# A decoder layer on one Trainium2 core: the indexer's small products on 64 rows, a weight split moved among the keys, a row sum moved ahead of a split

## The chip, the cores and the metric

The kernel runs on one core of one Trainium2 chip. The metric is device time in microseconds (us) of one execution; lower is better. The profile is that of one execution, taken by the hardware profiler. The engines are PE (TensorE, matrix products; PEld is its loading of weights), DVE (VectorE), ACT (ScalarE), POOL (GpSimd) and SP (SyncE, which issues the weights' transfers).

## The reference

One layer of a hybrid decoder on 256 tokens with 16 meta tokens ahead of them (T = 272), width 2048, all in float32. The parts that the change touches are the indexer, the keys and values, and the FFN's down projection with the last norm:

```python
q, c_kv, q_idx, k_idx, w_idx, u = split_columns(h @ w_in[l])
c_kv = rms_norm(c_kv, kv_norm_g[l])
...
dots = jnp.einsum('bqhd,bsd->bqhs', qi, k_idx)            # 16 indexer heads of 64
score = jnp.einsum('bqhs,bqh->bqs', jax.nn.relu(dots), wi)
_, sel = lax.top_k(score, top_k)                          # 64 of 272 keys
...
h = layer_norm(ALPHA * h + mix, ln1_g[l], ln1_b[l])
f = conv_gated_ffn(h, w_up[l], conv_w[l], conv_b[l], w_down[l])
h = layer_norm(ALPHA * h + f, ln2_g[l], ln2_b[l])
```

Attention then runs over the selected keys, and a causal pooling runs beside it; neither is touched.

## The kernel before

**Products in two parts.** Each fp32 operand is split into an upper part (rounded to fp32r, copied by ACT) and a lower part (the rest, subtracted by DVE). A product is three matmuls: upper weights by upper data (L199), upper by lower (L200) and lower by upper (L201), added up in PSUM. `product` issues them for 16 slices k of 128 rows.

**Weights.** The list `stream` (L92 to L104) holds all weight tiles of 128 x 2048 in the order of their use: eight tiles of the indexer's queries (two heads of 64 per tile), w_uk, w_uv, sixteen more projections, w_o, and the FFN's tiles by a plan; the last four are tiles of w_down (`spare` is the first of them, `last` the last). `weights(ahead=2)` hands out the next tile and calls `prefetch`, which calls `emit` (L135 to L158) for tiles two further on; `fetch` (L110 to L129) issues the transfer on SP and splits the tile in halves: ACT's upper (L127), DVE's lower (L128). The raw and the split tiles are in pools of three. Each engine works in the order in which its instructions are issued; where that isn't enough, `tc.issue_after` (in `behind`, L171 to L176) puts an instruction behind another one.

**Start.** 13 matmuls on zeros (L85 to L89; the zeros come from POOL) run while the first data comes. x and the first weights come in slices k, each split by ACT and DVE (L222 to L225), and L264 to L270 multiply them into three PSUM banks: indexer key and head weights (80 columns), and the two halves of the latent.

**Indexer.** The key of 64 rows is copied to both halves of `kidx`'s 128 rows (L273 to L279): slice 0 is the upper part on both halves, slices 1 and 2 are zero but for the lower part on one half each. The queries of a tile's two heads lie so (L383, L384) that head i has its upper part on half i of the rows and its lower part on the other half. One matmul of 128 rows with slice 0 therefore gives upper by upper and lower by upper, and one with slice 1 + i gives upper by lower:

```python
for o, n, t in ((pa_[:, S * i:S * i + S], S, slice(0, P)), (pb[:, :T], T, slice(P, S))):
    nc.tensor.matmul(o, qi[:, i, t], kidx[:, 0, :n], start=True, stop=False)
    nc.tensor.matmul(o, qi[:, i, t], kidx[:, 1 + i, :n], start=False, stop=True)
```

The queries are in two blocks of 128; the first sees 256 keys at most, the second 272. `dots(j)` does two heads; it is issued inside the product of the next tile, one head behind slice 9 and the other behind slice 12 (L369 to L385). ACT's relu and DVE's weighted sum turn it into `score`.

**Keys and values.** L394 to L403 multiply w_uk's tile with the latent into eight keys, each evicted by ACT (L401); dots(7) stands behind the third key. L407 to L439 multiply w_uv's tile into the values (L426 to L431). w_uv's tile is split like any other, two tiles ahead. DVE's top-k follows (L442 to L452).

**Last stage.** The last four tiles of w_down are split, and `row_sums` (L185 to L191) adds each raw tile's rows on ACT, in place, and splits the sum into two further columns of the split tile, from which PE makes the mean. L907 to L909 issue the row sums of the first three of them behind the third one's split. L984 to L1008 multiply the four tiles into pieces of the output: in each piece first tile 0, then tile 3, then tiles 1 and 2; the piece from 1792 on (MEAN) takes the sums' columns along. The partial results of the tiles before are added to y by DVE (L843), and L915 sums y.

Of the kernel before, what the change touches and what calls it, by code (L numbers as in the profile page):

```python
# [23 lines left out]
NQ = T - Q0  # L24
KT = D // P
# [4 lines left out]
DI = 64  # L30
# [13 lines left out]
KA = NM + P  # L44
# [24 lines left out]
def tile_layer(ctx, tc, xt, w_first, w_proj, w_uk, w_uv, w_pool, w_o, w_up, w_down, cols, rows, rel_bias, onehot, out):  # L69
    nc = tc.nc  # L70
# [10 lines left out]
    def small():  # L81
        return pa.tile([P, 512], F32, tag="at", name="at")


    warm = sb.tile([P, 256], mybir.dt.bfloat16, name="warm")  # L85
    nc.gpsimd.memset(warm, 0.0)
    ps = small()
    for _ in range(13):
        nc.tensor.matmul(ps[:, :256], warm[:, :P], warm, start=True, stop=True)  # L89


# [3 lines left out]
    kinds = {}  # L95
# [11 lines left out]
    ready, raws, split = {}, {}, {}  # L107
    state = {"next": 0, "use": 0}

    def fetch(raw, hl, src, kind, front):  # L110
# [15 lines left out]
        for c in (slice(a, b) for a, b in zip(cuts, cuts[1:])):  # L126
            upper = nc.scalar.activation(hl[:, 0, c], raw[:, c], AF.Copy)  # L127
            lower = nc.vector.tensor_tensor(hl[:, 1, c], raw[:, c], hl[:, 0, c].bitcast(F32), op=ALU.subtract)  # L128
        return tuple(getattr(ins, "ins", ins) for ins in (upper, lower))  # L129

    def weight_tiles():
        raw = wp.tile([P, 2048], F32, tag="wraw", name="wraw")
# [2 lines left out]
    def emit(i):  # L135
        if i in ready:
            return
        if i == last:

            raw = wp.tile([P, 2048], F32, tag="wraw", name="wraw")  # L140
            nc.sync.dma_start(raw, stream[i])
            raws[i] = raw
            ready[i] = []
            for c in range(0, 2048, 256):
                hl = ring.tile([P, 2, 258], F32R, tag="act", name="whl_r", padded_shape=[P, 2, T])
                nc.scalar.activation(hl[:, 0, :256], raw[:, c:c + 256], AF.Copy)
                nc.vector.tensor_tensor(hl[:, 1, :256], raw[:, c:c + 256], hl[:, 0, :256].bitcast(F32), op=ALU.subtract)
                ready[i].append(hl)
            return
        if i == spare:  # L150
            raw = wp.tile([P, 2048], F32, tag="wraw", name="wraw")
            hl = sb.tile([P, 2, 2048 + 2], F32R, tag="y", name="whl_y")
        else:
            raw, hl = weight_tiles()
        split[i] = fetch(raw, hl, stream[i], kinds.get(i), i and split[i - 1][1])
        ready[i] = hl
        if i >= spare:
            raws[i] = raw  # L158

# [25 lines left out]
    def row_sums(i, hl):  # L185

        total = sb.tile([P, 1], F32, name=f"total{i}")
        nc.scalar.activation(raws[i], raws[i], AF.Copy, accum_out=total)
        hi, lo = (hl[-1][:, p, 256:] if isinstance(hl, list) else hl[:, p, 2048:] for p in range(2))
        nc.scalar.activation(hi, total.to_broadcast([P, 2]), AF.Copy)  # L190
        nc.vector.tensor_tensor(lo, total.to_broadcast([P, 2]), hi.bitcast(F32), op=ALU.subtract)  # L191

    def product(ps, hl, m, act, lo, hi, ks=range(KT), width=P, k0=0, k1=KT):

        for n in range(k0, k1):
            k = ks[n]
            wh, wl = hl[:, 0, k * width:k * width + m], hl[:, 1, k * width:k * width + m]
            ah, al = act[k][:, 0, lo:hi], act[k][:, 1, lo:hi]
            nc.tensor.matmul(ps, wh, ah, start=n == 0, stop=False)  # L199
            nc.tensor.matmul(ps, wh, al, start=False, stop=False)  # L200
            nc.tensor.matmul(ps, wl, ah, start=False, stop=n == KT - 1)  # L201
# [61 lines left out]

    heads = [(big(), a, m) for a, m in ((0, 80), (80, P), (80 + P, P))]  # L264
    for k, (hl, a0) in enumerate(first):
        for ps, a, m in heads:
            wh, wl = hl[:, 0, a0 + a:a0 + a + m], hl[:, 1, a0 + a:a0 + a + m]
            nc.tensor.matmul(ps[:m, :T], wh, x_parts[k][:, 0, :], start=k == 0, stop=False)  # L268
            nc.tensor.matmul(ps[:m, :T], wh, x_parts[k][:, 1, :], start=False, stop=False)  # L269
            nc.tensor.matmul(ps[:m, :T], wl, x_parts[k][:, 0, :], start=False, stop=k == KT - 1)  # L270
    ps = heads[0][0]

    kidx = ap_.tile([P, 3, T], F32R, name="kidx", tag="kidx")  # L273
    nc.gpsimd.memset(kidx[:, 1:, :].bitcast(F32), 0.0)
    for r0 in (0, DI):
        nc.scalar.activation(kidx[r0:r0 + DI, 0, :], ps[:DI, :T], AF.Copy)
    for i in range(2):
        nc.vector.tensor_tensor(kidx[DI * i:DI * i + DI, 1 + i, :], ps[:DI, :T], kidx[:DI, 0, :].bitcast(F32),
                                op=ALU.subtract)  # L279
# [22 lines left out]
    ps = small()  # L302
# [46 lines left out]
            nc.gpsimd.dma_start(dst, src)  # L349


    def dots(j, qi, pa_, heads):

        for i in heads:
            h = 2 * j + i
            pb = small()
            for o, n, t in ((pa_[:, S * i:S * i + S], S, slice(0, P)), (pb[:, :T], T, slice(P, S))):
                nc.tensor.matmul(o, qi[:, i, t], kidx[:, 0, :n], start=True, stop=False)  # L358
                nc.tensor.matmul(o, qi[:, i, t], kidx[:, 1 + i, :n], start=False, stop=True)
# [9 lines left out]
    for j in range(8):  # L369
        hl = weights()  # L370
        ps = big()
        product(ps[:, :S], hl, P, x_parts, NM, T, k1=9)
        if j:
            pa_ = small()
            dots(j - 1, qis[j - 1], pa_, (0,))
        product(ps[:, :S], hl, P, x_parts, NM, T, k0=9, k1=12)
        if j:
            dots(j - 1, qis[j - 1], pa_, (1,))
        product(ps[:, :S], hl, P, x_parts, NM, T, k0=12)
        qi = queries[:, j % 2]  # L380
        for i in range(2):
            r, o = slice(DI * i, DI * i + DI), slice(DI - DI * i, 2 * DI - DI * i)
            nc.scalar.activation(qi[r, i, :], ps[r, :S], AF.Copy)  # L383
            nc.vector.tensor_tensor(qi[o, i, :], ps[r, :S], qi[r, i, :].bitcast(F32), op=ALU.subtract)  # L384
# [9 lines left out]
    for h in range(H):  # L394
        ps = small()
        for c in range(2):
            w = slice(1024 * c + h * HD, 1024 * c + h * HD + HD)
            nc.tensor.matmul(ps[:, :T], uk[:, 0, w], ctp[:, c, 0, :], start=c == 0, stop=False)
            nc.tensor.matmul(ps[:, :T], uk[:, 0, w], ctp[:, c, 1, :], start=False, stop=False)
            nc.tensor.matmul(ps[:, :T], uk[:, 1, w], ctp[:, c, 0, :], start=False, stop=c == 1)  # L400
        nc.scalar.activation(kt[:, h, :], ps[:, :T], AF.Copy)  # L401
# [515 lines left out]
    def piece(i, q):  # L917
        a, b = cuts[i][q]
# [165 lines left out]
```

## Time and profile before

| | |
|---|---|
| median of 3 runs | 1043.34 us (1043.13 to 1043.67) |
| the profiled execution | 1043.2 us, its span 1041.3 us |
| granted clock of PE, mean | 0.998 |
| ACT's splits of weights (L127) | 416, 402.8 us |
| DVE's lower parts (L128) | 416, 486.3 us |
| DMA | 250.28 MB, mean 240 GB/s |

The page gives each engine's busy time and its share of the span, then a chain of work that ended last, followed back from the end. A row of the timeline has the start in us from the span's start, the duration in us, the engine, the line, the operation, what it writes and reads, the shape, and how many instructions it stands for; behind these, in brackets, how long the engine stood idle before it and what ended that. A matmul's shape 128*128 128x256 is weights of 128 rows and 128 columns by data of 128 rows and 256 columns. Matmuls overlap in the pipeline and their ends are modelled, so the distance between two starts is the better measure of one matmul's slot.

### The profile page before, as it was taken

What the parts mean: (1) busy time and instruction counts of PE and PEld (TensorE: products, weight loads), DVE (VectorE), ACT (ScalarE), POOL (GpSimd) and SP (SyncE); (2) the same over time, 40 slices, a digit from 0 to 9 for tenths busy, and PEclk for the clock granted to TensorE, in tenths of its full rate; (3) what the DMA queues carried; (4) which work ended last, traced back from release to release, by engine and by line L of the source; (5) the groups of instructions that cost most, each with busy time, mean ns of one, the idle gap of its engine ahead of it and who ended that gap; (6) DMA issues with size and microseconds to landing.
All of it is one profiled execution on the core that took longest, in us unless ns stands there. A gap on an engine that the chain in (4) does not pass through costs nothing.

```text
span 1041.3 us, 19198 instructions
## 1 busy us (share of the span) xinstructions
PE 1033.3 (99%) x7643; PEld 984.3 (95%) x7643; DVE 891.0 (86%) x1401; ACT 621.0 (60%) x1000; POOL 189.5 (18%) x246
## 2 busy tenths in 40 slices
PE   9999999999999999999999999999999999999997
PEld 9999999999999999999999999999999999999986
DVE  6879568758779998888999999989998999999876
ACT  7656446645439855555665556555556565565665
POOL 1200014125330021130121111211112101120031
PEclk9999999999999999999999999999999999999999
DMA  9755543354553578879887788877988778887865
GB/s 326 259 187 218 214 142 131 134 200 165 176 189 131 197 223 240 278 282 302 274 277 261 269 297 276 276 263 267 296 271 285 264 274 285 279 273 271 288 215 160
DMA packets 59754, 250.28 MB, mean 240 GB/s; under 512 B 21734, under 2 KB 22416, under 8 KB 32656
## 3 DMA queue, kind: packets, MB, share of 16 engines
q1 hardware_dynamic: 34592, 230.42, 61.2%
q0 software_dynamic: 7888, 16.14, 8.3%
q10 hardware_dynamic: 17184, 2.49, 1.4%
q8 instruction: 60, 0.98, 0.4%
q14 instruction: 30, 0.25, 0.1%
HBM read 232.50 MB, written 2.11 MB: 225 GB/s over the span
## 4 chain that ended last, share of the span: by engine, by line
PE 89%; DVE 5%; issue 3%; ACT 1%; POOL 1%; DMA 1%; POOLq 0%; DVEq 0%; ACTq 0%
PE mm L200 22%; PE mm L199 22%; PE mm L201 22%; PE at L786 6%; PE at L785 6%; PE at L787 6%; DVE whl L128 2%; DMA wraw<-in_w_down 1%; PE mm L268 1%; PE mm L269 1%; PE mm L270 1%; ACT whl L127 1%; DVE x L701 0%; DVE hp L706 0%; PE at L358 0%
## 5 line engine op out<-in xcount | busy, mean ns | idle before, releaser
L128 DVE TENSOR_TENSOR whl<-wraw,whl 128x1024 fp32r<-128x1024 f32 (+1 forms) x416 | 486.3, 1203 | 37.7 <-ACT whl L127 36.8
L127 ACT ACTIVATE whl<-wraw 128x1024 fp32r<-128x1024 f32 (+1 forms) x416 | 402.8, 1015 | 98.6 <-PE mm L201 21.7
L200 PE MATMUL mm<-hp,whl 128*128 128x258 f32 x1280 | 362.4, 283 | 0.1
L199 PE MATMUL mm<-hp,whl 128*128 128x258 f32 x1280 | 361.4, 282 | 0.0
L201 PE MATMUL mm<-hp,whl 128*128 128x258 f32 x1280 | 361.2, 282 | 0.0
L200 PEld LDWEIGHTS mm<-hp,whl 128*128 128x128 f32 x1280 | 242.7, 190 | 3.3 <-DVE hp L706 0.3
L199 PEld LDWEIGHTS mm<-hp,whl 128*128 128x128 f32 x1280 | 242.5, 189 | 3.3
L201 PEld LDWEIGHTS mm<-hp,whl 128*128 128x128 f32 x1280 | 242.9, 190 | 0.2
L199 PE MATMUL mm<-xp,whl 128*128 128x256 f32 (+5 forms) x384 | 111.9, 291 | 0.0
L200 PE MATMUL mm<-xp,whl 128*128 128x256 f32 (+5 forms) x384 | 108.7, 283 | 0.0
L201 PE MATMUL mm<-xp,whl 128*128 128x256 f32 (+5 forms) x384 | 108.7, 283 | 0.0
L720 ACT ACTIVATE z<-mm,cv 128x256 f32<-128x256 f32 x40 | 22.6, 564 | 100.9 <-PE mm L201 100.9
L757 POOL TENSOR_TENSOR forms<-za 128x128 f32<-128x128 f32 x20 | 21.9, 1095 | 309.6 <-DVE za L738 243.1
L720 ACT ACTIVATE za<-mm,cv 128x256 f32<-128x256 f32 x40 | 22.6, 565 | 85.5 <-PE mm L201 77.4
L199 PEld LDWEIGHTS mm<-xp,whl 128*128 128x128 f32 x384 | 72.4, 189 | 1.0 <-issue 0.5
L200 PEld LDWEIGHTS mm<-xp,whl 128*128 128x128 f32 x384 | 72.3, 188 | 0.4
L201 PEld LDWEIGHTS mm<-xp,whl 128*128 128x128 f32 x384 | 72.4, 189 | 0.3 <-DVE whl L128 0.2
L786 PE MATMUL at<-whl,gp 128*128 128x512 f32 x180 | 71.1, 396 | 0.0
L787 PE MATMUL at<-whl,gp 128*128 128x512 f32 x180 | 71.0, 395 | 0.0
L785 PE MATMUL at<-whl,gp 128*128 128x512 f32 x180 | 69.3, 395 | 0.0
L760 POOL TENSOR_TENSOR forms<-za 128x128 f32<-128x128 f32 x20 | 22.6, 1131 | 199.0 <-DVE za L738 185.4
L787 PEld LDWEIGHTS at<-whl,gp 128*128 128x128 f32 x180 | 33.8, 188 | 7.9
(348 smaller groups left out, 1918.2 us busy)
## 6 DMA issues: line engine op xcount, KB each, us to landing
wraw<-in_w_up SPq DMA_DIRECT2D x88, 1024.0 KB, 5.0
wraw<-in_w_down SPq DMA_DIRECT2D x80, 1024.0 KB, 6.2
wraw<-in_w_proj SPq DMA_DIRECT2D x24, 1024.0 KB, 5.1
wraw<-in_w_o SPq DMA_DIRECT2D x16, 1024.0 KB, 4.9
y<-v POOLq DMA_DIRECT2D x27, 256.0 KB, 8.2
y<-u POOLq DMA_DIRECT2D x18, 256.0 KB, 4.9
wraw<-in_w_first SPq DMA_DIRECT2D x8, 304.0 KB, 5.4
x<-in_xt SPq DMA_DIRECT2D x1, 2176.0 KB, 8.4
```

The lines of the kernel that those rows point to most:

```text
L127: upper = nc.scalar.activation(hl[:, 0, c], raw[:, c], AF.Copy)
L128: lower = nc.vector.tensor_tensor(hl[:, 1, c], raw[:, c], hl[:, 0, c].bitcast(F32), op=ALU.subtract)
L199: nc.tensor.matmul(ps, wh, ah, start=n == 0, stop=False)
L200: nc.tensor.matmul(ps, wh, al, start=False, stop=False)
L201: nc.tensor.matmul(ps, wl, ah, start=False, stop=n == KT - 1)
L268: nc.tensor.matmul(ps[:m, :T], wh, x_parts[k][:, 0, :], start=k == 0, stop=False)
L720: nc.scalar.activation(z, src[:, 2:NQ], AF.Identity, bias=col(C_B, j), scale=col(C_W, 3 * j + 2))
L757: nc.gpsimd.tensor_tensor(s[:, 0], a21, a22, op=ALU.add)
L760: nc.gpsimd.tensor_tensor(s[:, 3], a11, a21, op=ALU.subtract)
L785: nc.tensor.matmul(ps, a[:, 0, i], hl[:, 0, w], start=j == 0, stop=False)
L786: nc.tensor.matmul(ps, a[:, 0, i], hl[:, 1, w], start=False, stop=False)
L787: nc.tensor.matmul(ps, a[:, 1, i], hl[:, 0, w], start=False, stop=j == n - 1)
```

## The change

- **Indexer.** `kidx` has two slices, upper and lower, both filled on both halves. `dots` takes four PSUM banks, issues the four upper products on 128 rows and then four lower products on 64 rows each, the first head's on rows 0 to 63 and the second's on rows 64 to 127. Both heads stand behind slice 9 of the next tile. dots(7) takes its banks from the other pool.
- **Values' weights.** At w_uv's place in the stream only its transfer is issued. Its split is done in halves, behind the evictions of the second and the fourth key; the keys' evictions stand behind the last query's.
- **Row sum.** The row sum of the first of the last four tiles is issued ahead of the second tile's split, which is put behind it; the sums over y stand behind the last row sum.
- **Start.** The warm-up reads a constant of the program, not POOL's zeros, and has 14 matmuls. For the first four slices the three banks' products are ordered by kind: all upper by upper, then upper by lower, then lower by upper.

The diff, without the lines that only pass these things on:

```diff
-    warm = sb.tile([P, 256], mybir.dt.bfloat16, name="warm")
-    nc.gpsimd.memset(warm, 0.0)
+    warm = nc.const_aps.tensor(1.0, (P, 256), mybir.dt.bfloat16)
     ps = small()
-    for _ in range(13):
+    for _ in range(14):
...
+    def split_part(raw, hl, c, after=()):
+        with ExitStack() as edges:
+            for ins in after:
+                edges.enter_context(tc.issue_after(ins))
+            upper = nc.scalar.activation(hl[:, 0, c], raw[:, c], AF.Copy)
+        lower = nc.vector.tensor_tensor(hl[:, 1, c], raw[:, c], hl[:, 0, c].bitcast(F32), op=ALU.subtract)
+        return tuple(getattr(ins, "ins", ins) for ins in (upper, lower))
...
-        split[i] = fetch(raw, hl, stream[i], kinds.get(i), i and split[i - 1][1])
         ready[i] = hl
+        if i == VALUES:
+
+            nc.sync.dma_start(raw, stream[i])
+            held.extend((raw, hl))
+            return
+        if i == spare + 1:
+
+            with behind(spare):
+                sums = row_sums(spare, ready[spare])
+            split[i] = fetch(raw, hl, stream[i], None, 0, (sums,))
+        else:
+            split[i] = fetch(raw, hl, stream[i], kinds.get(i), i and i - 1 in split and split[i - 1][1])
...
-        for ps, a, m in heads:
-            wh, wl = hl[:, 0, a0 + a:a0 + a + m], hl[:, 1, a0 + a:a0 + a + m]
-            nc.tensor.matmul(ps[:m, :T], wh, x_parts[k][:, 0, :], start=k == 0, stop=False)
-            nc.tensor.matmul(ps[:m, :T], wh, x_parts[k][:, 1, :], start=False, stop=False)
-            nc.tensor.matmul(ps[:m, :T], wl, x_parts[k][:, 0, :], start=False, stop=k == KT - 1)
+
+        terms = [(t, h) for h in heads for t in range(3)]
+        if k < 4:
+            terms.sort(key=lambda x: x[0])
+        for t, (ps, a, m) in terms:
+            nc.tensor.matmul(ps[:m, :T], hl[:, t // 2, a0 + a:a0 + a + m], x_parts[k][:, t % 2, :],
+                             start=k == 0 and t == 0, stop=k == KT - 1 and t == 2)
...
-    kidx = ap_.tile([P, 3, T], F32R, name="kidx", tag="kidx")
-    nc.gpsimd.memset(kidx[:, 1:, :].bitcast(F32), 0.0)
+    kidx = ap_.tile([P, 2, T], F32R, name="kidx", tag="kidx")
...
+    for r0 in (0, DI):
+        nc.vector.tensor_tensor(kidx[r0:r0 + DI, 1, :], ps[:DI, :T], kidx[:DI, 0, :].bitcast(F32), op=ALU.subtract)
...
-    def dots(j, qi, pa_, heads):
-
-        for i in heads:
+    def dots(j, qi, buffer=small):
+
+
+        ps = [[buffer(), buffer()] for _ in range(2)]
+
+        blocks = ((S, slice(0, P)), (T, slice(P, S)))
+        for i2, (n, t) in enumerate(blocks):
+            for i in range(2):
+                nc.tensor.matmul(ps[i2][i][:, :n], qi[:, i, t], kidx[:, 0, :n], start=True, stop=False)
+        for i2, (n, t) in enumerate(blocks):
+            for i in range(2):
+                r = slice(DI * i, DI * i + DI)
+                nc.tensor.matmul(ps[i2][i][:, :n], qi[r, i, t], kidx[r, 1, :n], start=False, stop=True)
+        for i in range(2):
             h = 2 * j + i
-            pb = small()
-            for o, n, t in ((pa_[:, S * i:S * i + S], S, slice(0, P)), (pb[:, :T], T, slice(P, S))):
-                nc.tensor.matmul(o, qi[:, i, t], kidx[:, 0, :n], start=True, stop=False)
-                nc.tensor.matmul(o, qi[:, i, t], kidx[:, 1 + i, :n], start=False, stop=True)
             rl = temp([P, KW], "rl")
-            nc.scalar.activation(rl[:, :KA], pa_[:, S * i:S * i + KA], AF.Relu)
-            nc.scalar.activation(rl[:, KA:], pb[:, :T], AF.Relu)
             for i2, (a, b) in enumerate(((0, KA), (KA, KW))):
+                nc.scalar.activation(rl[:, a:b], ps[i2][i][:, :b - a], AF.Relu)
...
         product(ps[:, :S], hl, P, x_parts, NM, T, k1=9)
         if j:
-            pa_ = small()
-            dots(j - 1, qis[j - 1], pa_, (0,))
-        product(ps[:, :S], hl, P, x_parts, NM, T, k0=9, k1=12)
-        if j:
-            dots(j - 1, qis[j - 1], pa_, (1,))
-        product(ps[:, :S], hl, P, x_parts, NM, T, k0=12)
+            dots(j - 1, qis[j - 1])
+        product(ps[:, :S], hl, P, x_parts, NM, T, k0=9)
...
-        nc.scalar.activation(kt[:, h, :], ps[:, :T], AF.Copy)
+        with tc.issue_after(query):
+            key = nc.scalar.activation(kt[:, h, :], ps[:, :T], AF.Copy)
         if h == 2:
-            dots(7, qis[7], small(), (0, 1))
+            dots(7, qis[7], big)
+        if h in (1, 3):
+
+            split_part(*held, slice(512 * h - 512, 512 * h + 512), (getattr(key, "ins", key),))
...
     with behind(spare + n - 2):
-        for k in range(n - 1):
-            row_sums(spare + k, hls[k])
+        for k in range(1, n - 1):
+            of_weights = row_sums(spare + k, hls[k])
...
     for i in range(2):
-        nc.scalar.activation(y2[:, i], y2[:, i], AF.Copy, accum_out=mvs[i][:, 0:1])
+        with tc.issue_after(of_weights):
+            nc.scalar.activation(y2[:, i], y2[:, i], AF.Copy, accum_out=mvs[i][:, 0:1])
```

More of the change, by code (lines that the diff above doesn't have):

```diff
@@ L106, in tile_layer, with fetch @@
     spare, last = len(stream) - PARTS[-1], len(stream) - 1
-    ready, raws, split = {}, {}, {}
+    VALUES = stream.index(w_uv)
+    ready, raws, split, held = {}, {}, {}, []
     state = {"next": 0, "use": 0}
-    def fetch(raw, hl, src, kind, front):
+    def split_part(raw, hl, c, after=()):
[5 more added lines that the diff above has]
+        return tuple(getattr(ins, "ins", ins) for ins in (upper, lower))
+    def fetch(raw, hl, src, kind, front, after=()):
         nc.sync.dma_start(raw, src)
@@ L125, in fetch @@
             cuts = (0, 1024, 1536)
[L126 to L129, printed above, removed]
+        for a, b in zip(cuts, cuts[1:]):
+            parts = split_part(raw, hl, slice(a, b), after)
+        return parts
     def weight_tiles():
@@ L189, in row_sums @@
         hi, lo = (hl[-1][:, p, 256:] if isinstance(hl, list) else hl[:, p, 2048:] for p in range(2))
-        nc.scalar.activation(hi, total.to_broadcast([P, 2]), AF.Copy)
+        upper = nc.scalar.activation(hi, total.to_broadcast([P, 2]), AF.Copy)
         nc.vector.tensor_tensor(lo, total.to_broadcast([P, 2]), hi.bitcast(F32), op=ALU.subtract)
+        return getattr(upper, "ins", upper)
     def product(ps, hl, m, act, lo, hi, ks=range(KT), width=P, k0=0, k1=KT):
@@ L265, in tile_layer @@
     for k, (hl, a0) in enumerate(first):
-        for ps, a, m in heads:
-            wh, wl = hl[:, 0, a0 + a:a0 + a + m], hl[:, 1, a0 + a:a0 + a + m]
-            nc.tensor.matmul(ps[:m, :T], wh, x_parts[k][:, 0, :], start=k == 0, stop=False)
-            nc.tensor.matmul(ps[:m, :T], wh, x_parts[k][:, 1, :], start=False, stop=False)
-            nc.tensor.matmul(ps[:m, :T], wl, x_parts[k][:, 0, :], start=False, stop=k == KT - 1)
+        terms = [(t, h) for h in heads for t in range(3)]
[4 more added lines that the diff above has]
+                             start=k == 0 and t == 0, stop=k == KT - 1 and t == 2)
     ps = heads[0][0]
-    kidx = ap_.tile([P, 3, T], F32R, name="kidx", tag="kidx")
-    nc.gpsimd.memset(kidx[:, 1:, :].bitcast(F32), 0.0)
+    kidx = ap_.tile([P, 2, T], F32R, name="kidx", tag="kidx")
     for r0 in (0, DI):
         nc.scalar.activation(kidx[r0:r0 + DI, 0, :], ps[:DI, :T], AF.Copy)
-    for i in range(2):
-        nc.vector.tensor_tensor(kidx[DI * i:DI * i + DI, 1 + i, :], ps[:DI, :T], kidx[:DI, 0, :].bitcast(F32),
-                                op=ALU.subtract)
+    for r0 in (0, DI):
+        nc.vector.tensor_tensor(kidx[r0:r0 + DI, 1, :], ps[:DI, :T], kidx[:DI, 0, :].bitcast(F32), op=ALU.subtract)
     wt = temp([P, S], "wt")
@@ L382, in tile_layer @@
             r, o = slice(DI * i, DI * i + DI), slice(DI - DI * i, 2 * DI - DI * i)
-            nc.scalar.activation(qi[r, i, :], ps[r, :S], AF.Copy)
+            query = nc.scalar.activation(qi[r, i, :], ps[r, :S], AF.Copy)
+            query = getattr(query, "ins", query)
             nc.vector.tensor_tensor(qi[o, i, :], ps[r, :S], qi[r, i, :].bitcast(F32), op=ALU.subtract)
```

## The prediction

> **What bounds the kernel now.** I read the page first (busy shares, the chain that ended last), then the timeline of PE and of its weight loads around the indexer, then the timelines of ACT, DVE and PE in the keys' stage and in the last stage.
>
> ```profile
> span 1041.3 us, 19198 instructions
> PE 1033.3 (99%) x7643; PEld 984.3 (95%) x7643; DVE 891.0 (86%) x1401; ACT 621.0 (60%) x1000; POOL 189.5 (18%) x246
> PE 89%; DVE 5%; issue 3%; ACT 1%; POOL 1%; DMA 1%; POOLq 0%; DVEq 0%; ACTq 0%
> ```
>
> PE is busy 99% of the span and 89% of the chain is PE. So an edit moves the time only where it changes how many matmul slots PE needs, or opens or closes a gap between them. Ends of matmuls are modelled, so I go by starts. All sums are made against the profiled execution, 1043.2 us (span 1041.3 and 1.9 around it); it is 0.14 below the median of the runs, 1043.34.
>
> **Indexer products: what goes.** One head's scores before:
>
> ```profile
> 33.33 0.28 PE L358 MATMUL at<-kidx,qi 128*128 128x256 f32 x1
> 33.45 0.28 PE L359 MATMUL at<-kidx,qi 128*128 128x256 f32 x1
> 33.69 0.29 PE L359 MATMUL at<-kidx,qi 128*128 128x272 f32 x1
> 33.82 0.28 PE L199 MATMUL mm<-xp,whl 128*128 128x256 f32 x1
> ```
>
> Four matmuls take 33.33 to 33.82, that is 0.49; the two of L359 are half of it, about 0.243 (0.118 at 256 columns, 0.125 at 272). Each of the eight `dots` has two heads, so its four lower products take 0.486. On 64 rows the two heads' products lie on different halves of the array. If a pair takes the time of one, a `dots` saves 0.243. In the changed program order dots(2) to dots(7) issue four upper products and then four lower ones. In dots(0) one lower product stands alone among the upper ones and three come later; in dots(1) three come first and one alone later. Each of these two has only one pair and two stretches of 64-row work. That makes 14 pairs, 14 × 0.1215 = 1.70 saved at most, and 10 stretches.
>
> **Indexer products: what comes.** No 64-row matmul is in the trace. The nearest rows are matmuls on fewer rows between 128-row ones, and two controls:
>
> ```profile
> 38.10 0.28 PE L201 MATMUL mm<-xp,whl 128*128 128x256 f32 x1
> 38.31 0.09 PEld L339 LDWEIGHTS at<-oh,rb_sb 32*8 32x8 f32 x2
> 38.86 0.19 PEld L199 LDWEIGHTS mm<-xp,whl 128*128 128x128 f32 x1 [0.46 <-issue]
> 38.97 0.19 PEld L200 LDWEIGHTS mm<-xp,whl 128*128 128x128 f32 x1
> ...
> 25.55 0.28 PE L199 MATMUL mm<-xp,whl 128*128 128x256 f32 x1
> 26.21 0.28 PE L201 MATMUL mm<-xp,whl 128*128 128x256 f32 x1
> ...
> 29.05 0.28 PE L201 MATMUL mm<-xp,whl 128*128 128x256 f32 x1
> 29.06 0.79 PEld L246 LDWEIGHTS at<-sq,ones 128*128 128x128 f32 x4
> ...
> 85.59 0.28 PE L400 MATMUL at<-ctp,whl 128*128 128x272 f32 x1
> 85.59 0.12 PEld L426 LDWEIGHTS at<-whl,few 128*48 128x48 f32 x1
> ```
>
> Normally a load starts with the matmul ahead of it and is hidden: so at 29.06, also for plain fp32 (L246), and at 85.59 for fewer columns (L426). Ahead of the 32-row matmul of L339 it does not: L201 starts at 38.10, streams 0.12, and the load starts at 38.31, 0.21 after it. So fewer rows, not the type, go with the wait. On the way back the load of L199 starts at 38.86 and the next one, which starts with L199's matmul, at 38.97: 0.11 of load is in the open.
>
> One stretch then costs, going in, the 0.09 of waiting (0.21 − 0.12) and a load of 128 columns in the open, 0.11; and coming out as much again, 0.09 and 0.11: 0.39. Bounds: the two loads alone are 0.22; from above, the 16-row transposes (L304) between L199 at 25.55 and L201 at 26.21 leave 0.66 − 0.24 = 0.42 with their own passes in it. From below, if 64 rows count as a full shape, as L426's columns do, a stretch costs nothing. I take 0.39, since L339 and L304 are the rows with fewer rows, and keep 0 and 0.42 for the range. Then a clean `dots` costs 0.39 − 0.243 = +0.15, six of them +0.88. dots(0) and dots(1) cost 4 × 0.39 − 2 × 0.1215 = +1.32 together. Sum **+2.2**.
>
> The Trainium skill, "TensorEngine Tiling (Array Packing)", Key Properties, says that changing the tiling mode drains TensorE and that tiles load and multiply independently of each other; its Theoretical Speedup gives up to 2 times for a contraction of 64. The L339 rows agree with the drain, no row shows the doubling, and by the doubling without a drain the sum would be that of the first rival.
>
> **Waits at dots.** With both heads at k = 9 the second head is needed nine products of 0.118 (1.1) sooner than before. The last query parts for dots(6):
>
> ```profile
> 73.72 0.43 DVE L384 TENSOR_TENSOR qi<-mm,qi 64x256 fp32r<-64x256 f32 x1
> 74.03 0.28 PE L358 MATMUL at<-kidx,qi 128*128 128x256 f32 x1
> ```
>
> DVE ends at 74.15, and PE would now want it at 74.15 too, for the second upper product (74.03 + 0.12). Behind a late query stands everything that PE still has to do, since it works in order. I take +0.1 over the seven places, from 0 to 0.35.
>
> **Values' weights among the keys.** Before, two ACT splits of 1024 columns stand between the last queries and the first key evictions:
>
> ```profile
> 77.49 0.28 PE L398 MATMUL at<-ctp,whl 128*128 128x272 f32 x1
> 80.39 0.39 PE L201 MATMUL mm<-xp,whl 128*128 128x258 f32 x1
> 81.04 0.39 PE L358 MATMUL at<-kidx,qi 128*128 128x272 f32 x1
> 85.71 0.39 PE L426 MATMUL at<-whl,few 128*48 128x512 f32 x1
> ...
> 78.03 1.04 ACT L127 ACTIVATE whl<-wraw 128x1024 fp32r<-128x1024 f32 x1
> 79.10 0.38 ACT L383 ACTIVATE qi<-mm 64x256 fp32r<-64x256 f32 x1
> 79.51 1.06 ACT L127 ACTIVATE whl<-wraw 128x1024 fp32r<-128x1024 f32 x1
> 80.59 0.98 ACT L401 ACTIVATE kt<-at 128x272 f32<-128x272 f32 x3
> ```
>
> The stage lasts 77.49 to 85.71, 8.22. In it lie 48 key matmuls of 0.125 (6.0), dots(7) (0.97) and four product matmuls (0.48): 7.45. So **0.77** is gaps; PE wants an "at" bank that the eviction at 80.59 had not freed. Afterwards the two query parts (0.38 each) and two key evictions (0.33 each) come first on ACT; one half of the split (1.04) follows the second key's eviction, the other the fourth's. Adding these up in ACT's new order, the "mm" bank that dots(7)'s fourth upper product wants is free near 79.5, 0.6 before its slot, and the second half's lower part is done near 84.7, 0.4 before the values want it. I take −0.77; if either is late, the gain shrinks to 0.
>
> **Start.** The changed order of terms and the constant for the warm-up meet this:
>
> ```profile
> 9.20 0.51 DVE L225 TENSOR_TENSOR whl<-wraw,whl 128x336 fp32r<-128x336 f32 x1
> 9.76 0.35 PE L270 MATMUL mm<-xp,whl 128*80 128x272 f32 x1
> ```
>
> PE waits there for DVE's lower part, which ends at 9.71, whatever came before. This follows the arrival of data, which the edit leaves alone. Value 0, from −0.4 to +0.3.
>
> **Last stage: the row sum ahead of the next split.**
>
> ```profile
> 997.24 1.92 ACT L188 ACTIVATE wraw<-wraw 128x2048 f32<-128x2048 f32 x1 [0.23 <-DVE whl_r L147]
> 999.28 0.20 ACT L190 ACTIVATE whl_r<-total 128x2 fp32r<-128x2 f32 x1
> 1002.69 2.36 DVE L128 TENSOR_TENSOR whl_y<-wraw,whl_y 128x1024 fp32r<-128x1024 f32 x2 [1.95 <-ACT whl_y L127]
> 1006.43 2.02 ACT L127 ACTIVATE whl<-wraw 128x1024 fp32r<-128x1024 f32 x2 [2.83 <-DMA wraw<-in_w_down]
> 1007.53 2.36 DVE L128 TENSOR_TENSOR whl<-wraw,whl 128x1024 fp32r<-128x1024 f32 x2 [2.48 <-ACT whl L127]
> 1009.81 0.68 DVE L843 TENSOR_TENSOR y<-y,mm 128x512 f32<-128x512 f32 x1
> 1010.40 1.22 DVE L128 TENSOR_TENSOR whl<-wraw,whl 128x1024 fp32r<-128x1024 f32 x1
> 1011.88 0.39 PE L992 MATMUL mm<-whl,gp 128*128 128x512 f32 x1
> 1019.01 0.28 PE L991 MATMUL mm<-whl,gp 128*128 128x258 f32 x1
> 1019.49 0.39 PE L992 MATMUL mm<-whl,gp 128*128 128x258 f32 x1 [0.20 <-DVE whl L191]
> ```
>
> The sum overwrites the raw tile, so it waits for DVE to end the spare tile's lower part, 1002.69 + 2.36 = 1005.05. It takes 2.2 (997.24 to 999.28 and L190): ACT is free at 1007.25, the next split starts there and not at 1006.43. Its lower part moves by the same 0.82 and ends at 1010.7, not 1009.9. Behind it DVE now does both additions to y (0.6 each) ahead of the last lower part, where it did one: that part's first half ends near 1013.0 (before 1011.6). PE wants it at 1011.88 + 0.23 (one matmul of the next piece has been put ahead) = 1012.1: a new gap of **0.9**. In return the row sum that holds PE at 1019.49 (0.48 after its forerunner, where 0.12 is the rule, and 0.1 more behind it) is early: **−0.48**. Sum **+0.4**, from −0.48 (no gap) to +0.8. Everything behind hangs on PE's last piece and moves with it.
>
> **Sum.** 2.2 + 0.1 − 0.77 + 0 + 0.4 = +1.9, so 1043.2 + 1.9 = **1045.1**.
>
> **The rivals.**
> 1. Side by side without a drain (the other side: faster). For it: L426 changes the shape without a wait, and no 64-row matmul contradicts it; against it L339 and L304. Then −1.7 + 0.1 − 0.77 + 0.4 = −2.0, **1041.2**; without the gap in the last stage (−0.48 in place of +0.4) **1040.3**. It decides from a stretch of under 0.20 on: at 10 × 0.20 the 1.7 saved and the 0.27 of the other terms are spent.
> 2. Drain, and the two halves load one after the other. Loads of 0.11 then set the pace of the four lower products: 0.39 + 3 × 0.107 + 0.125 − 0.486 = +0.35 for a clean `dots`, six make 2.1; dots(0) and dots(1) save nearly nothing and cost 1.5. 3.6 + 0.1 − 0.77 + 0.4 = +3.3, **1046.5**. For it: at 38.97 the next load starts 0.11 after the one before, never sooner.
> 3. The change doesn't do what it says: 64-row matmuls neither overlap nor drain and keep 0.12 apart. Then 0 + 0.1 − 0.77 + 0.4 = −0.3, **1042.9**.
>
> **How the numbers follow.** 0.2% is 2.09 us, about what a measurement of this kernel can tell from no change; around the median that is 1041.25 to 1045.43. My forecast has 0.38; rival 1 has 0.36, since both rows against it have at most 32 rows; rival 2 0.14; rival 3 0.12. Each spreads by some 0.9 from the keys' stage, the last stage and the start. Faster: 0.26 of rival 1 and 0.01 of rival 3, 0.27. Slower: 0.18 of the forecast (which lies just under the bound), 0.13 of rival 2, 0.01 of rival 3, 0.32. The rest, 0.41, is the same. Both signs hold much of the chance, so the range must reach to rival 1: 1040.0 (rival 1 with the gain in the last stage and 0.3 at the start) to 1047.0 (rival 2 with 0.5 more of waits). The forecast's own range is 1044.2 to 1046.0.
>
> **What would show it.** Indexer: the load of the first 64-row product starts about 0.21 after the last upper product (drain) or with it (rival 1); starts of a pair lie close together (side by side) or 0.11 to 0.12 apart (rivals 2 and 3); 0.2 is lost again on the way back. Keys: from the first key to the first values' matmul about 7.1 (7.45 without the four product matmuls, which the new order puts elsewhere, and 0.15 for dots(7)), no gap near 80. Last stage: a gap of 0.9 near 1012 ahead of the third tile's lower products and none in the mean's piece near 1019. Start: L270's counterpart still at 9.7. I am wrong if 64-row stretches cost under 0.20, or if a gap opens at a place that this sum leaves at nothing.

## The result

The changed kernel takes 1048.62 us in the median of 6 runs, the kernel before 1043.62 in the median of 6 beside it: 5.0 us slower, a ratio of 1.0046 (95% interval 1.0036 to 1.0056). Forecast were 1045.1 and a range that ended at 1047.0. The page of the changed kernel (profiled execution 1049.5 us):

```profile
span 1047.6 us, 19182 instructions
PE 1038.0 (99%) x7644; PEld 983.9 (94%) x7644; DVE 892.9 (85%) x1401; ACT 619.9 (59%) x1000; POOL 184.6 (18%) x244
PE 82%; DVE 8%; DMA 4%; issue 3%; ACT 1%; POOL 1%; SPq 0%; POOLq 0%; DVEq 0%; ACTq 0%
```

PE is as full as before, yet its share of the chain fell from 89% to 82%: more of the path leads through DVE and through transfers. The shares don't say where. For that I laid the PE starts of the two traces beside each other, section by section. Since one execution of each is thin, both kernels were traced a second time (e11 and e12 below). The columns of the two kernels have the first and the second trace, in us from the start of one product to the start of another. Forecast is the prediction's sum, taken apart by section; measured compares the second traces, whose spans, 1041.6 and 1046.6, lie 5.0 apart like the medians:

| section, by PE's starts | before | changed | forecast | measured |
|---|---|---|---|---|
| start to the first query tile | 23.07, 23.88 | 23.24, 23.68 | 0 | −0.20 |
| first two slices of that tile | 0.71, 0.71 | 1.07, 1.40 | 0 | +0.69 |
| rest of that tile | 6.15, 6.15 | 6.12, 6.12 | 0 | −0.03 |
| second tile, with dots(0) | 6.86, 6.86 | 8.53, 7.50 | +0.66 | +0.64 |
| third tile, with dots(1) | 7.43, 7.43 | 8.27, 8.11 | +0.66 | +0.68 |
| five tiles with dots(2) to dots(6) | 33.27, 33.28 | 34.95, 34.93 | +0.83 | +1.65 |
| keys, dots(7), values, to the tenth projection | 20.93, 20.95 | 20.37, 20.37 | −0.62 | −0.58 |
| on to the FFN's first product on `hp` | 251.70, 251.71 | 251.85, 251.84 | 0 | +0.13 |
| FFN, first to last product on `hp` | 634.83, 634.85 | 635.48, 635.48 | 0 | +0.63 |
| on to the last four tiles | 24.58, 24.58 | 24.56, 24.56 | 0 | −0.02 |
| last four tiles, first to last product | 22.83, 22.35 | 24.29, 23.63 | +0.4 | +1.28 |
| to the end | 8.96, 8.87 | 8.90, 8.98 | 0 | +0.11 |

Four rows carry the miss of 3.1: dots(2) to dots(6) with 0.8 above the forecast, the last four tiles with 0.9, the FFN with 0.6 and the first tile with 0.7. One `dots` of the changed kernel (its timeline, PE, PEld and DVE) answers to the rows of L358 and L359:

```profile
56.99 0.43 DVE L406 TENSOR_TENSOR qi<-mm,qi 64x256 fp32r<-64x256 f32 x1
57.25 0.28 PE L220 MATMUL mm<-xp,whl 128*128 128x256 f32 x1
57.25 0.70 PEld L379 LDWEIGHTS at<-kidx,qi 128*128 128x128 f32 x4
57.37 0.80 PE L379 MATMUL at<-kidx,qi 128*128 128x256 f32 x4
57.88 0.29 PE L379 MATMUL at<-kidx,qi 128*128 128x272 f32 x1
58.10 0.30 PEld L383 LDWEIGHTS at<-kidx,qi 64*128 64x128 f32 x4
58.10 0.51 PE L383 MATMUL at<-kidx,qi 64*128 64x256 f32 x4
58.54 0.39 PE L218 MATMUL mm<-xp,whl 128*128 128x256 f32 x1
58.65 0.19 PEld L219 LDWEIGHTS mm<-xp,whl 128*128 128x128 f32 x1
```

The four loads of L379 are one row there. A view of a narrower window has the second of them, the second head's query, by itself:

```profile
57.53 0.19 PEld L379 LDWEIGHTS at<-kidx,qi 128*128 128x128 f32 x1
```

Two things are to be seen. The 64-row stretch: the last upper product starts at 57.88, the first 64-row load at 58.10, 0.22 later; the four loads and the four products then take two slots and not four; the way back puts the first real product at 58.65, where the next load starts. From 57.88 + 0.125 to 58.65 are 0.64, against 0.486 for four lower products on 128 rows: +0.15, as forecast. And the uppers: from 57.37 to 57.88 + 0.125 are 0.64, where four of 0.12 take 0.486. That is a second 0.15 which the forecast doesn't have. The load of the second head's query was due with the first upper product at 57.37, DVE had that query ready at 57.42 (56.99 + 0.43), and the load starts at 57.53.

### The profile page after: what moved, and what is told of

Same layout as the page of the kernel before. It is cut to its first block, busy times and chain, and to the rows that moved or that the text cites. A ratio compares the mean times of both kernels' runs of the same rounds, so it can differ in the third digit from the quotient of the medians.

```text
span 1047.6 us, 19182 instructions
## 1 busy us (share of the span) xinstructions
PE 1038.0 (99%) x7644; PEld 983.9 (94%) x7644; DVE 892.9 (85%) x1401; ACT 619.9 (59%) x1000; POOL 184.6 (18%) x244
## 4 chain that ended last, share of the span: by engine, by line
PE 82%; DVE 8%; DMA 4%; issue 3%; ACT 1%; POOL 1%; SPq 0%; POOLq 0%; DVEq 0%; ACTq 0%
PE mm L218 21%; PE mm L219 21%; PE mm L220 20%; PE at L811 5%; PE at L812 5%; PE at L813 5%; DVE whl L115 3%; DMA wraw<-in_w_down 2%; DMA wraw<-in_w_first 1%; DMA wraw<-in_w_proj 1%; ACT whl L114 1%; DVE x L727 0%; DVE hp L732 0%; PE mm L518 0%; PE at L379 0%
## 5 line engine op out<-in xcount | busy, mean ns | idle before, releaser
L783 POOL TENSOR_TENSOR forms<-za 128x128 f32<-128x128 f32 x20 | 21.3, 1063 | 311.4 <-DVE za L764 244.8
L786 POOL TENSOR_TENSOR forms<-za 128x128 f32<-128x128 f32 x20 | 20.8, 1041 | 199.7 <-DVE za L764 185.8
```

What stands on the lines that cost most here:

```text
L783: nc.gpsimd.tensor_tensor(s[:, 0], a21, a22, op=ALU.add)
L786: nc.gpsimd.tensor_tensor(s[:, 3], a11, a21, op=ALU.subtract)
```

## The experiments

Times are medians in us, before is the kernel before on the same chip in the same job. Where a version is compared with the changed kernel, that is the 1048.62 above unless another is named. The two were measured in different jobs, and each one's distance from the kernel before is known to about 1 us either way, so the finer readings go by sections of the traces. The reasons under test: **the waits** (the second head's query part comes late), **the stretches** (going in and out of the 64-row shape), and **the last stage**.

**e1, the scores behind slice 12.**

```diff
-        product(ps[:, :S], hl, P, x_parts, NM, T, k1=9)
+        product(ps[:, :S], hl, P, x_parts, NM, T, k1=12)
         if j:
             dots(j - 1, qis[j - 1])
-        product(ps[:, :S], hl, P, x_parts, NM, T, k0=9)
+        product(ps[:, :S], hl, P, x_parts, NM, T, k0=12)
```

> The changed kernel with both heads' scores behind slice 12 of the next tile, not behind slice 9; everything else kept. Theory of the waits: PE stands still at the second upper product until the second head's query part is there (1.2 us at dots(0) and about 0.155 at each of dots(2) to dots(6), 2.0 together, in the trace of the changed kernel). Behind slice 12 the part has 1.06 us more, so these gaps close; dots(0) also becomes one stretch of 64-row work in place of two. About 2.2 us less than the changed kernel, some 1046.4. Rival, the stretches: the excess lies in entering and leaving the 64-row shape, which all but one stay: at most 0.3 less, some 1048.3.

1047.15, before 1043.66 (ratio 1.0033, 1.0021 to 1.0046): 1.5 less than the changed kernel, where 2.2 was expected. The same `dots` there:

```profile
55.82 0.42 DVE L406 TENSOR_TENSOR qi<-mm,qi 64x256 fp32r<-64x256 f32 x1
57.12 0.54 PEld L379 LDWEIGHTS at<-kidx,qi 128*128 128x128 f32 x4
57.24 0.65 PE L379 MATMUL at<-kidx,qi 128*128 128x256 f32 x4
```

The query is 0.9 early now, and the four loads take 0.54, not 0.70: 0.16 a place is the wait. The five tiles with dots(2) to dots(6) lie 6.78 to 6.84 apart, 0.13 to 0.16 above the kernel before: what is left is the price of the clean stretch alone. Part of the gain is lost in dots(1): its fourth upper product wants a bank that holds the relative bias until DVE's copy ends (43.91 + 0.43), and starts 0.54 behind its forerunner (the bracket counts 0.15 of that, from the forerunner's modelled end). That tile takes 8.51 here, against 8.27 and 8.11 in the changed kernel.

```profile
43.91 0.43 DVE L361 COPY strip<-at 8x272 f32<-8x272 f32 x1
44.39 0.39 PE L379 MATMUL at<-kidx,qi 128*128 128x272 f32 x1 [0.15 <-DVE strip L361]
```

**e2, the lower products on 128 rows.**

```diff
-    kidx = ap_.tile([P, 2, T], F32R, name="kidx", tag="kidx")
+    kidx = ap_.tile([P, 3, T], F32R, name="kidx", tag="kidx")
+    nc.gpsimd.memset(kidx[:, 1:, :].bitcast(F32), 0.0)
...
-                r = slice(DI * i, DI * i + DI)
-                nc.tensor.matmul(ps[i2][i][:, :n], qi[r, i, t], kidx[r, 1, :n], start=False, stop=True)
+                nc.tensor.matmul(ps[i2][i][:, :n], qi[:, i, t], kidx[:, 1 + i, :n], start=False, stop=True)
```

> The changed kernel with its lower products on 128 rows again, by the two slices that are zero on the other half (filled as before the change); order of issue and everything else kept. Theory of the stretches: entering and leaving costs 0.39 each for 10 stretches, 3.9, of which 1.7 comes back from 14 pairs side by side; without them 2.2 us less, some 1046.4, and the waits for the second head's query stay in the trace at 1.2 and about 0.155. Rival: the stretches cost nothing net and the whole excess in the indexer is the waits: no change from the changed kernel, 1048.6.

1046.67, before 1043.66 (1.0030, 1.0020 to 1.0039): 1.95 less than the changed kernel; the net loss of the stretches is there. The tiles with dots(2) to dots(6) still take 0.15 to 0.22 more than before, 0.94 together: the waits without the stretches. At dots(0) it shows no wait; the tile with dots(1) takes 7.83, 0.40 more than before, and waits for the same bank as in e1.

**e3, the indexer as before.** The functions and lines of the indexer from the kernel before, the rest as changed.

> The changed kernel with the whole indexer part as before (scores of the two heads behind slices 9 and 12, 128 rows, zeros); values' weights, row sum and start as changed. If waits (2.0) and stretches (2.2) add up, 4.2 us less than the changed kernel, some 1044.4, and what is left against the kernel before is the keys' gain of 0.6 to 0.8 and the last stage's loss of 0.5 to 1.4. Rival: the last stage and the start carry most of the loss: still 1046 or more.

1044.67, before 1043.66 (1.0015, 1.0006 to 1.0024): 3.95 less. By this difference the indexer part is four fifths of the loss (alone, in e13, it costs 2.5); its tiles lie 6.65 to 6.68 apart as before.

**e4, the row sum as before.**

```diff
-        if i == spare + 1:
-
-            with behind(spare):
-                sums = row_sums(spare, ready[spare])
-            split[i] = fetch(raw, hl, stream[i], None, 0, (sums,))
...
-        for k in range(1, n - 1):
+        for k in range(n - 1):
```

> The changed kernel with the row sums of the last four tiles issued as before the change; everything else kept. Theory: the early sum delays the next split, and PE waits about 1 to 1.8 us at the third of these tiles, while the mean's piece wins 0.48: without it 0.5 to 1.4 us less, some 1047.5, and no gap in PE there. Rival: the gap follows the arrival of these tiles and stays: 1048.6 or, with the wait of the mean's piece back, 1049.1.

1046.66, before 1043.66 (1.0028, 1.0017 to 1.0040): 1.96 less, more than expected. The last four tiles take 23.32 in its trace, 0.3 to 1.0 less than in those of the changed kernel. The gap at the third tile is gone, and the mean's piece waits again, 0.9 in all. The second tile takes 7.50 with the same indexer, so the 8.53 of the first trace of the changed kernel is no fixed cost.

**e5, the values' part alone; e6, with the start.** On the kernel before, the split of w_uv's tile among the keys and the order of the evictions; in e6 also the constant, the 14 matmuls and the order of the first slices.

> The kernel before with one part of the change alone: the values' weights split among the keys, and the keys' evictions behind the last query's. Theory: the gaps of the keys' stage go, 0.6 to 0.77 us less than before, some 1042.9. Rival, from the traces so far: every trace with the change has 0.65 us more between the FFN's first and last up product than the trace of before; if this part brings that, no gain, 1043.6.

> The kernel before with the values' part and the changed start (constant for the warm-up, order of the first four slices); indexer and row sum as before. Theory: the start is worth nothing, the same as with the values alone, some 1042.9. Rival: the start's part moves something that costs through the whole kernel (the 0.65 us in the FFN): 1043.5. From the sums of e3 and e4 against the changed kernel (1048.6 - 3.95 - 1.96) comes 1042.7.

1044.24 and 1043.76, before 1043.62 (1.0005, 0.9996 to 1.0014; 1.0001, 0.9992 to 1.0010): no gain in either. In e5 the keys' stage wins 0.63 (8.22 to 7.59), the stretch behind it, to the tenth projection, gives 0.26 back (12.71 to 12.97), and the FFN takes 0.63 more. The rival of e5 was right; that of e6, by which the start brings the longer FFN, was not, since e5 has it without the start. First and last product on `hp`, second trace of before, then e5:

```profile
350.96 0.28 PE L199 MATMUL mm<-hp,whl 128*128 128x258 f32 x1
985.81 0.28 PE L201 MATMUL mm<-hp,whl 128*128 128x258 f32 x1
```

```profile
350.60 0.28 PE L213 MATMUL mm<-hp,whl 128*128 128x258 f32 x1
986.07 0.28 PE L215 MATMUL mm<-hp,whl 128*128 128x258 f32 x1
```

634.85 and 635.47, though the instructions between are the same and in the same order. No single gap makes it: no distance between two starts differs by more than 0.02, and the difference builds up along the stretch. PE's mean distance from one matmul of 258 columns to the next is 120.16 ns in place of 120.10 (3764 of them, 0.23 us), from one of 512 columns to the next 233.33 in place of 232.83 (672 of them, 0.33 us); the rest lies where the two alternate. The granted clock doesn't differ: it is 1.00 there in both.

**e7, two stretches for one.**

```diff
         for i2, (n, t) in enumerate(blocks):
             for i in range(2):
                 nc.tensor.matmul(ps[i2][i][:, :n], qi[:, i, t], kidx[:, 0, :n], start=True, stop=False)
-        for i2, (n, t) in enumerate(blocks):
             for i in range(2):
```

> The changed kernel with each block's two lower products right behind its two upper ones: the pairs stay, the program order now has 18 stretches of 64-row work, not 10 (dots(0) and dots(1) three, the others two). Theory: a stretch costs 0.39 for going in and out, so 8 more cost 3.1, some 1051.7, and each stretch in the trace starts 0.21 after its forerunner. Rival: the cost is per dots or in the waits for the queries alone: no change, 1048.6.

1051.44, before 1043.62 (1.0077, 1.0065 to 1.0090): 2.8 more than the changed kernel, of 3.1 expected. The tiles take 7.33 to 7.41 in place of 6.94 to 7.04: 0.37 to 0.41 for a further stretch.

**e8, both heads on the same half.**

```diff
-                r = slice(DI * i, DI * i + DI)
+                r = slice(0, DI)
```

> The changed kernel with both heads' lower products on rows 0 to 63. The second head's are then computed from its query's lower part, so that head's scores are changed; number and shape of the matmuls are not. Theory: pairs on different halves run side by side; on the same half each takes its own slot of 0.12, 14 x 0.1215 = 1.7 us more, some 1050.3, and the starts in a pair lie 0.12 apart, not 0.003. Rival: the small distance is a matter of 64-row work as such and not of the halves: no change, 1048.6.

1049.44, before 1043.62 (1.0057, 1.0045 to 1.0070). Against the 1048.62 of the changed kernel that is 0.8 and not 1.7, and against its second set of runs (1048.27, e12) 1.2; but this trace has no late first tile (0.71, not 1.07 or 1.40). Tile by tile it is clear: 7.18 to 7.26 where the changed kernel takes 6.94 to 7.04, 0.22 to 0.26 more, the 0.243 of two pairs. The four products spread from 0.51 to 0.74:

```profile
56.98 0.74 PE L383 MATMUL at<-kidx,qi 64*128 64x256 f32 x4
```

So the halves do run side by side, and only as different halves.

**e9, the early row sum without its wait.** The sum's copy goes to the split tile that is filled next, not over its raw tile.

```diff
-        nc.scalar.activation(raws[i], raws[i], AF.Copy, accum_out=total)
+        nc.scalar.activation(raws[i] if out_ is None else out_, raws[i], AF.Copy, accum_out=total)
...
-                sums = row_sums(spare, ready[spare])
+                sums = row_sums(spare, ready[spare], hl[:, 0, :2048])
```

> The changed kernel with the early row sum's copy written not over its raw tile but into the split tile that is filled next, so that the sum need not wait for DVE's last reading of the raw tile. Theory of the last stage: the loss is that wait, 1.4 us during which ACT is free; the sum then fits ahead of the next split, the gap of PE at the third tile goes and the mean's piece keeps its gain: from PE's first product of the last four tiles to its last 22.4 us (24.29 in the changed kernel, 22.83 before), 1.9 us less than the changed kernel. Rival: the next split is late whatever the sum does (its transfer lands late): the stage stays at 23.3 or more.

1047.03, before 1043.36 (1.0036, 1.0023 to 1.0049); the changed kernel in the same job took 1048.27 (e12). The last four tiles take 22.43, as expected, and 23.63 there. ACT's timeline in e9 and then, with DVE and PE, in the second trace of the changed kernel:

```profile
1006.43 2.01 ACT L114 ACTIVATE whl_y<-wraw 128x1024 fp32r<-128x1024 f32 x2 [2.69 <-DMA wraw<-in_w_down]
1008.35 1.90 ACT L206 ACTIVATE whl<-wraw 128x2048 fp32r<-128x2048 f32 x1
1010.48 3.89 ACT L114 ACTIVATE whl<-wraw 128x1024 fp32r<-128x1024 f32 x4
```

```profile
1006.17 2.01 ACT L114 ACTIVATE whl_y<-wraw 128x1024 fp32r<-128x1024 f32 x2 [2.21 <-DMA wraw<-in_w_down]
1009.66 1.92 ACT L206 ACTIVATE wraw<-wraw 128x2048 f32<-128x2048 f32 x1 [1.48 <-DVE whl_y L115]
1011.80 3.90 ACT L114 ACTIVATE whl<-wraw 128x1024 fp32r<-128x1024 f32 x4
1015.18 1.27 DVE L869 TENSOR_TENSOR y<-y,mm 128x512 f32<-128x512 f32 x2
1016.38 2.35 DVE L115 TENSOR_TENSOR whl<-wraw,whl 128x1024 fp32r<-128x1024 f32 x2
1016.32 0.39 PE L1018 MATMUL mm<-whl_y,gp 128*128 128x512 f32 x1
1017.65 0.50 PE L1019 MATMUL mm<-whl,gp 128*128 128x512 f32 x1 [0.94 <-DVE whl L115]
```

In the changed kernel ACT stands 1.48 for DVE, sums, and the next splits start at 1011.80; DVE does both additions to y ahead of the last lower part, and PE, which issued its last matmul at 1016.32, gets it at 1017.65 (a distance of 1.33, of which 0.23 is the matmul). In e9 the sum follows the split at once, and the two splits start 4.05 behind the spare tile's, not 5.63.

**e10, the parts that win, together.** e6 with e9's row sum.

> The kernel before with the values' part, the start and the early row sum written to the next split tile; the indexer as before. If the parts add up: the keys' stage and what follows it 0.3 less than before, the last stage 0.4 less, 0.7 us faster than before, some 1042.9. Rival: the 0.65 us more in the FFN that all traces with the change show eat it: 1043.6.

1043.55, before 1043.36 (1.0005, 0.9996 to 1.0014). The last four tiles take 22.44, the FFN 635.47. As its rival had it, the longer FFN eats the gain. No version beats the kernel before.

**e11 and e12, both kernels once more.**

> The kernel before once more, for a second trace of it. If the 0.65 us between the FFN's first and last up product (634.83 in the first trace of before, 635.48 in all traces with the change) lie in the run and not in the kernel, this trace shows 635.5 too; if they lie in the change, 634.8. The time is that of before either way, 1043.6.

> The changed kernel once more, for a second trace of it. In the first one the second head's query at dots(0) came 1.2 us late, behind a split whose transfer landed late, while the kernel with the old row sum, whose indexer is the same, lost there 0.2 only. If this wait hangs on the arrival of the transfer, it is another one now, and tile 1 to tile 2 takes between 7.5 and 8.5 us; if it belongs to the order of the instructions alone, 8.5 again. The gaps of about 0.15 at dots(2) to dots(6) are there either way. Time 1047.6 to 1049.6.

1043.70 (before 1043.36; 1.0002, 0.9993 to 1.0010) and 1048.27 (1.0045, 1.0033 to 1.0058). The 634.8 belong to the kernel before. In the first trace of the changed kernel PE had stood 0.96 at dots(0), since ACT's query part stands behind a split whose transfer was late; the second trace has no such wait and takes 7.50:

```profile
32.55 1.06 ACT L114 ACTIVATE whl<-wraw 128x1024 fp32r<-128x1024 f32 x1 [2.18 <-DVE r L270]
33.64 0.38 ACT L404 ACTIVATE qi<-mm 64x256 fp32r<-64x256 f32 x1
34.90 0.43 DVE L406 TENSOR_TENSOR qi<-mm,qi 64x256 fp32r<-64x256 f32 x1
35.39 0.39 PE L379 MATMUL at<-kidx,qi 128*128 128x256 f32 x1 [0.96 <-DVE qi L406]
```

The bracket names DVE's transpose, on which the split doesn't depend; its own wait is for the transfer, which the trace has landing at 32.47. In the second trace it lands at 30.79, and in e1, e2 and e4 the same split starts at 30.41 to 30.46.

**e13, e14, e15: the indexer, the start and the row sum, each alone** on the kernel before, without the values' part.

> The kernel before with the indexer part alone (64 rows, both heads behind slice 9); values, row sum and start as before. Theory: stretches 2.2, the late queries at dots(2) to dots(6) 0.9, so 3.1 more than before, some 1046.6, and 634.8 in the FFN, since the longer FFN goes with the values' part. Rival: the first weight tile of the queries is late with this part (0.4 to 1.0 us more there in seven of eight traces with it, in one of the seven without): then 3.6 to 4.1 more, some 1047.3.

> The kernel before with the changed start alone (constant for the warm-up, 14 matmuls, order of the first four slices). Theory: nothing, 1043.5, and 634.8 in the FFN. Rival: the constant moves every tile behind it by 512 bytes, and that makes the FFN's slots longer: 635.5 there and 1044.1.

> The kernel before with the early row sum alone (over its raw tile, as in the change). Theory: the last four tiles take 23.6 us as in the changed kernel against 22.4 to 22.8, so 0.8 to 1.3 more than before, some 1044.6, and 634.8 in the FFN. Rival: the loss needs the later arrival of these tiles that the changed kernel had: 22.8 and 1043.5.

1046.19, 1044.25 and 1044.48, before 1043.69 (1.0023, 1.0014 to 1.0032; 1.0001, 0.9992 to 1.0010; 1.0004, 0.9995 to 1.0012). The FFN takes 634.84, 634.86 and 634.85: the 0.63 belong to the values' part. The indexer alone costs 2.5 (3.1 expected), with dots at 7.50 and 8.12 and five tiles at 35.0 as in the changed kernel, and it has the late first tile (1.17). The row sum alone takes 23.51 in the last four tiles; its time moved by 0.8, which its interval doesn't tell from nothing. All traces together do: with the old sums these tiles take 22.35 to 23.32 (seven traces), with the early sum over its raw tile 23.51 to 24.32 (eight), with the early sum written elsewhere 22.43 and 22.44. The start alone shows no change of the time.

## Why the prediction was wrong

- **The stretches (+2.2): right.** Going in and out costs 0.39 and the pairs give back 0.243 a `dots`: dots(0) and dots(1) measured +1.32 for +1.32, a clean `dots` +0.15 for +0.15 (e1), a further stretch 0.37 to 0.41 (e7), a lost pair 0.12 (e8). The Trainium skill, "TensorEngine Tiling (Array Packing)", says in Key Properties that a change of tiling mode drains TensorE and that tiles work independently: both show here, as 0.22 ahead of the first load and as pairs that share a slot. The doubling of its Theoretical Speedup holds for the slots, and the way in and out takes more than it gives when a stretch has four products.
- **Waits at dots (+0.1): the first step that failed; it measures 0.9.** I compared the end of DVE's query part (74.15) with the start of the matmul that uses it (74.15). But the query is that matmul's weights, and the load that takes it would start a slot earlier, with the matmul ahead (74.03): it is 0.12 late. In the changed kernel's first trace the query comes 0.05 to 0.11 after its load was due, at each of dots(2) to dots(6), and the load starts another 0.12 after that. e1, where the wait is gone, and e2, where it alone is left, each show 0.14 to 0.22 a place, five places, 0.9.
- **Values among the keys (−0.77): right at its place, and given back elsewhere.** The −0.58 of the table has dots(7)'s stretch in it, for which e2 shows 0.18. But the gain needs two parts of the change: with dots(7) as before (e3, e5) only about 0.4 is won up to the tenth projection, and another 0.35 comes with the new dots(7) (20.19 in e2, 20.54 in e3). Whether its banks or its order bring it was not tried. The FFN's 0.63 was a term that the sum did not have. e5, e13, e14 and e15 tie it to the values' part. Why the same instructions run 0.1% slower there stays open; nothing was tried beyond leaving the part out.
- **The last stage (+0.4): the mechanism was right, the size not.** It measures +1.28 between the second traces, and 1.2 between the means of all traces (24.0 with the early sum over its raw tile, 22.8 with the old sums). Two sizes failed, both read from one execution. The gap was to be 0.9, from a spare tile whose split starts 7.9 ahead of the stage's first product; the three traces with such a tile (7.8 to 7.9) have gaps of 1.1 to 1.2, of which 0.1 is a slow first matmul behind the gap, and the five in which it comes 7.1 to 7.3 ahead have 1.7 to 1.9. The wait of the mean's piece, which was to give back 0.48, differs as much: five of the seven traces with the old sums have 0.3 to 0.9 of it, the second trace of before and e13 none. It grows with the start of the third tile's split, 2.3 to 0.2 ahead of the stage's first product.
- **The start (0): measured −0.20 and +0.69.** Over all traces the time to the first query tile is 23.0 to 24.9 with the changed start and 23.1 to 23.9 without, so the −0.20 is scatter; the kernel with the start alone has no late slice (0.71). The late slice goes with the indexer part (eight of its nine traces, and one of the eight others). In the nine traces that have it the split of the first weight tile starts at 21.4 to 22.3, in the others at 20.6 to 21.1. Why that tile's transfer lands later stays open: it happens before the first `dots`.
- **The rivals.** The one on the other side, side by side without a drain, fell with the 0.22. Loads one after the other (1046.5) came nearer in time, but for another reason: the loads of a pair start together. The third, which neither overlaps nor drains, fell with both.

## What to carry to other kernels

A reduced-row product pays only when a stretch is long enough to earn its way in and out: here 0.39 against 0.12 a pair, so by these numbers at least four pairs in a stretch (two are the most that ran here). An operand that PE loads as weights is due one matmul earlier than the matmul that uses it, and a wait that hangs on when a transfer lands differs from one execution to the next (0 to 0.9 us for the mean's piece), so what closing it is worth has to be read from several traces. Writing a side result over an input makes it wait for the last reader of that input; written into a tile that is overwritten next, it cost no wait here.

## What was not expected of the hardware

The same FFN instructions took 634.83 to 634.86 us in the five traces without the values' part and 635.47 to 635.49 in the twelve with it: a difference of 0.1% that repeats to 0.03, has no gap to point to and no difference of the granted clock beside it.
